# First mixer's window attention in plain fp32 on halves of TensorE's array, instead of in split fp32r pairs

## The chip, the cores and the metric

One core of one Trainium2 chip runs the whole program. The metric is the device time of one execution in microseconds (us). The kernel's engines are TensorE (PE, with its weight loads listed as PEld), VectorE (DVE), ScalarE (ACT), GpSimd (POOL) and SyncE (SP, which issues most of the DMAs).

## The reference, cut to what matters

The program is an encoder of two layers on 1024 tokens of width 1024. The first layer's token mixer is an attention in a window: 16 query heads of width 64, in four groups of four that share one key head and one value head, with a learned sink per head.

```python
def window_gqa_sink(q, k, v, sink):
    ...   # blocks of 128 tokens; each sees its own block and the one on either side (band 384)
    s = jnp.einsum('bnqhgd,bnkhd->bnhgqk', qb, kb, preferred_element_type=F32) * (d ** -0.5)
    ...
    s = jnp.where(valid[None, :, None, None], s, -jnp.inf)
    m = jnp.maximum(jnp.max(s, axis=-1, keepdims=True), sk)
    p = jnp.exp(s - m)
    p = p / (jnp.sum(p, axis=-1, keepdims=True) + jnp.exp(sk - m))
    o = jnp.einsum('bnhgqk,bnkhd->bnqhgd', p.astype(v.dtype), vb)

def mixer_window_attn(u, mem_kv, w_in, sink, w_out, pos):
    q, k, v, xq = jnp.split(u @ w_in, [...], axis=-1)
    q, k = rope(q), rope(k)
    o = window_gqa_sink(q, k, v, sink)
    return jnp.concatenate([o, memory_cross_attn(xq, mem_kv)], axis=-1) @ w_out
```

After the mixer come an output projection, a gated feed-forward part, and the second layer (a gated linear recurrence, here called `hgrn`, and another feed-forward part). All arithmetic is asked for in float32.

## The kernel before

The kernel computes float32 products on TensorE in a cheaper type, F32R, by splitting: a tile x becomes a high part h (x cast to F32R, by ACT) and a low part l = x - h (by DVE). `split` does this. `mm3` then forms h*h + h*l + l*h in three matmuls. Lines 83, 84 and 85 are these three matmuls wherever they are used, lines 88 and 89 the two halves of `split`, and lines 78 and 79 those of the weights in `wunit`. A matmul takes a stationary operand (its weight load is an instruction of its own in the trace) and streams a moving operand through it. A matmul on plain F32 tiles stands in the trace as two MATMUL records, one on F32R tiles and a transpose as one.

`window()` runs the first mixer. For each of the four groups g, `proj(g)` projects eight token tiles (`token(t)`, 24 matmuls of 384 columns each into `pj`), applies the rotation on DVE and POOL into `rq`, and turns `rq` by transposes into `ptq` (`turn`), from which the query tiles `qs` and the key tiles are made. `attend(g)` then takes eight blocks of 128 tokens. For each block and each of its four heads it forms scores in a PSUM tile `ps` (two buffers), adds the mask and takes the maximum on DVE into `sm`, takes the exponential on ACT, scales the rows by the reciprocal of the sum, transposes `sm` chunk by chunk into `pt` (two buffers), moves that to SBUF, and multiplies it with the values into `po` (one buffer). A block in the middle has 384 keys (three chunks), the first and last have 256 (two), which gives 22 chunks for a group and 88 in all. Between them run the units of the cross attention (`cross_unit`), which use the same PSUM tiles.

In the kernel before, both products of the window attention use split operands in a packed form. For the scores, a query tile holds the high part of a head on 64 rows and its low part on the other 64, the key tiles `kh` and `kl` hold the key twice, and two matmuls over all 128 rows (lines 374 and 375) give one head's scores. For the values, `v` holds the high part in 64 columns and the low part in the next 64, `ph` and `pl` are the two parts of the transposed probabilities of four heads (512 columns), and two matmuls per chunk (lines 399 and 400) give `po`, whose two halves ACT and DVE add into `o` (lines 402 and 403).

The output of groups 0 to 2 is written to DRAM (`oT`) and read back later by the output projection. That of group 3 goes by DMA into `ul` and is split from there (`split_moved`). The output projection's first part (`wo0.begin`, matmuls into `pb`) is laid beside `attend(3)`.

The order of instructions on each engine comes from a scheduler that orders the program by its own estimate of times when it is built. `tc.high_priority(n)` puts an instruction ahead of others in it, and `tc.issue_after(x)` keeps an instruction behind x. TensorE executes its matmuls in the order the scheduler gave. In `hgrn`, the lines `pe.matmul(pa[i:i + 32, c, j:j + n], ..., tile_position=(0, i))` (line 1222) already use a part of the array: 128 rows by 32 columns, in plain fp32.

Of the kernel before, what the change touches and what calls it, by code (L numbers as in the profile page):

```python
# [18 lines left out]
P = 128  # L19
# [30 lines left out]
def build(tc, A, out):  # L50
# [195 lines left out]
    def window():  # L246
# [8 lines left out]
        ap_.tile([64, 4, 256], F32, tag="o", bufs=2, name="o")  # L255
        for x, n in (("kh", 1), ("kl", 1), ("v", 1), ("qs", 8), ("ph", 2), ("pl", 2)):
            if x == "v":
                ap_.tile([P, NT, P], F32R, tag=x, bufs=n, name=x)
            else:
                ap_.tile([P, 512 if n > 1 else T], F32R, tag=x, bufs=n, name=x)  # L260
# [13 lines left out]
        def proj(g):  # L274
            us = [wunit(A["wqkv"][g, u], 768, eng=pool if u < QKV_POOL[g] else None) for u in range(4)]
            qs = [[None] * 2 for _ in range(4)]
            kvp = ap_ if g % 2 else ea
            kh = kvp.tile([P, T], F32R, tag="kh", bufs=1, name="kh")
            kl = kvp.tile([P, T], F32R, tag="kl", bufs=1, name="kl")
            v = kvp.tile([P, NT, P], F32R, tag="v", bufs=1, name="v")  # L280
            def token(t):
# [19 lines left out]
                cast = act.activation(v[:, t, :64], ps[:, 320:], AF.Copy, scale=rs0[:, t:t + 1])  # L301
                if g == 0 and t + 5 < NT:
                    tag = ("kh", "kl", "v")[t]
                    row = ap_.tile([P, NT, P] if tag == "v" else [P, T], F32R, tag=tag, bufs=1, name="row").bitcast(F32)
                    row = row.rearrange("p a b -> p (a b)") if tag == "v" else row
# [28 lines left out]
            kept = (qs, kh, kl, v)  # L334
# [12 lines left out]
        marks, moved = {}, []  # L347

        def split_moved():
            ts_ = moved.pop()  # L350
            oh, ol = uh[:, 6:8, ts_], ul[:, 6:8, ts_]
            act.copy(oh, ol.bitcast(F32))
            dve.tensor_tensor(ol, ol.bitcast(F32), oh.bitcast(F32), op=ALU.subtract)

        def attend(g, qkv, blocks=range(NT)):
            qs, kh, kl, v = qkv
            for b in range(2):
                for nn in range(4):
# [3 lines left out]
                    if nn % 2 == 0:  # L362
                        pairs[0] = ap_.tile([64, 4, 256], F32, tag="o", bufs=2, name="o")
                    o = pairs[0]
# [5 lines left out]
                    pool.tensor_copy(sm[:, :, w:w + 1], sk[:, 4 * g:4 * g + 4].unsqueeze(2))  # L370
                    for j in range(4):
                        s = psp.tile([P, 384], F32, tag="ps", bufs=2, name="ps")
                        m = slice(nn * P, (nn + 1) * P)
                        pe.matmul(s[:, :w], qs[j][b][:, m], kh[:, lo * P:hi * P], start=True, stop=False)
                        pe.matmul(s[:, :w], qs[j][b][:, m], kl[:, lo * P:hi * P], start=False, stop=True)
                        hd = 4 * g + j
                        dve.tensor_tensor_reduce(out=sm[:, j, :w], in0=s[:, :w], in1=wmask[:, mo:mo + w],
                                                 scale=-0.125, scalar=sk[:, hd:hd + 1], op0=ALU.add, op1=ALU.min,
                                                 accum_out=st["nm"][:, j:j + 1])
# [3 lines left out]
                    if moved and n % 2 == 0:  # L383
                        with tc.issue_after(marks[g, n].ins):
                            split_moved()
                    dve.reciprocal(st["rd"], st["su"])
                    for j in range(4):
                        if j < 2:
# [3 lines left out]
                    po = psp.tile([P, 4, P], F32, tag="po", bufs=1, name="po")  # L392
                    for c in range(hi - lo):
# [3 lines left out]
                        ph, pl = pair("p", c)  # L397
                        split(ph, pl, tp.rearrange("p a b -> p (a b)"))
                        pe.matmul(po, v[:, lo + c, :], ph, start=c == 0, stop=False)
                        pe.matmul(po, v[:, lo + c, :], pl, start=False, stop=c == hi - lo - 1)  # L400
                    ov = o[:, :, (nn % 2) * P:(nn % 2 + 1) * P]
                    act.copy(ov, po[64:])
                    dve.tensor_tensor(ov, po[:64], ov, op=ALU.add)
                    if nn % 2 == 1 and g == 3:
                        ts_ = slice((n - 1) * P, (n + 1) * P)
                        moved.append(ts_)
                        for hp in range(2):
                            nc.sync.dma_start(ul[hp * 64:(hp + 1) * 64, 6:8, ts_].bitcast(F32), o[:, hp::2, :])
                        if n == NT - 1:
                            split_moved()  # L410
                    elif nn % 2 == 1:
                        ts_ = slice((n - 1) * P, (n + 1) * P)
                        for hp in range(2):
                            nc.sync.dma_start(
                                oT[0][2 * g:2 * g + 2, hp * 64:(hp + 1) * 64, ts_].rearrange("a d t -> d a t"),
                                o[:, hp::2, :])
# [1166 lines left out]
```

## Time and profile before

| what | value |
|---|---|
| time, median of 3 runs | 2644.66 us (2641.44 to 2646.29) |
| the profiled execution, its span | 2644.4 us |
| PE busy over the span | 2598.7 us (98%) |
| DVE, ACT, POOL busy | 1807.8 us (68%), 1379.0 us (52%), 486.7 us (18%) |
| granted TensorE clock over 40 slices | 9 tenths or more in each |

The span of the profiled execution is 0.3 us under the median of the runs shown, so sums made against the one hold for the other. Busy time of PE is modelled from start to end of each matmul, and matmuls overlap, so the distance from one start to the next tells what a matmul costs in a stream. The window attention's own matmuls lie between 83.7 us and 493 us of the span, and the profile's views are asked for that stretch.

### The profile page before, as it was taken

Reading aid. Unit: us, or ns where it says so; the run is one execution under the profiler, and the core shown is the slowest. Engines: PE = TensorE matmul, PEld = TensorE weight load, DVE = VectorE, ACT = ScalarE, POOL = GpSimd, SP = SyncE. Lnnn points to the kernel's source line nnn. Section 1 sums busy time; section 2 is a strip of 40 time slices with the busy share of each in tenths; the row PEclk is TensorE's granted clock in tenths of the full one; section 3 lists DMA queues with packets and bytes.
Section 4 is the critical chain, followed back from the end, with each engine's and each line's share of the span. In section 5 each row is a group of like instructions: output and inputs, shape, how many; then the busy total and the mean of one; then the engine's idle time right before and its main releaser. Section 6 shows DMA issues by size and latency. Waiting matters only on the chain. (4 is left out here: it accounts for less than half of the span.)

```text
span 2644.4 us, 38978 instructions
## 1 busy us (share of the span) xinstructions
PE 2598.7 (98%) x14420; PEld 2187.7 (83%) x14420; DVE 1807.8 (68%) x2875; ACT 1379.0 (52%) x2471; POOL 486.7 (18%) x552
## 2 busy tenths in 40 slices
PE   8999999999999999999999999999999999999998
PEld 8988887887888888887888888888887788888887
DVE  6778777587656565488688686887757665656447
ACT  6667767445444444455465554555534444444443
POOL 0421120221111100032234131231311111110013
PEclk9999999999999999999999999999999999999999
DMA  9782232367877757673236351103337777785666
GB/s 354 248 191 46 74 102 69 126 190 187 210 200 197 198 158 251 201 258 127 85 112 162 85 119 47 54 32 116 121 113 191 197 196 203 202 206 166 219 193 236
DMA packets 195726, 425.92 MB, mean 161 GB/s; under 512 B 20048, under 2 KB 56272, under 8 KB 189904
## 3 DMA queue, kind: packets, MB, share of 16 engines
q1 hardware_dynamic: 161552, 324.06, 38.0%
q0 software_dynamic: 24544, 90.19, 16.5%
q10 hardware_dynamic: 9440, 9.19, 1.0%
q8 instruction: 113, 1.85, 0.3%
q14 instruction: 77, 0.63, 0.1%
HBM read 330.04 MB, written 116.39 MB: 169 GB/s over the span
## 5 line engine op out<-in xcount | busy, mean ns | idle before, releaser
L89 DVE TENSOR_TENSOR wl<-st,wh 128x1024 fp32r<-128x1024 f32 (+1 forms) x238 | 262.8, 1111 | 318.0 <-ACT wh L88 291.5
L88 ACT CAST wh<-st 128x1024 fp32r<-128x1024 f32 (+1 forms) x238 | 222.1, 935 | 286.1 <-PE X L588 186.4
L83 PE MATMUL pj<-uh,wh 128*128 128x512 f32 x512 | 202.5, 396 | 3.4 <-DVE q L1139 2.0
L588 PE MATMUL X<-wl,wh 128*128 128x512 f32 x528 | 204.7, 389 | 0.3 <-DVE wl L89 0.3
L588 PE MATMUL X<-wh,wl 128*128 128x512 f32 x528 | 204.5, 389 | 0.0
L85 PE MATMUL pj<-uh,wl 128*128 128x512 f32 x512 | 202.3, 395 | 0.0
L84 PE MATMUL pj<-ul,wh 128*128 128x512 f32 x512 | 200.9, 392 | 0.1
L588 PE MATMUL X<-wh 128*128 128x512 f32 x528 | 198.7, 390 | 0.3 <-ACT c L1002 0.3
L83 PE MATMUL pj<-wh,uh 128*128 128x384 f32 (+1 forms) x512 | 189.5, 371 | 3.7 <-DVE gs L1125 2.4
L84 PE MATMUL pj<-wl,uh 128*128 128x384 f32 (+1 forms) x512 | 187.2, 366 | 0.0
L85 PE MATMUL pj<-wh,ul 128*128 128x384 f32 (+1 forms) x512 | 187.2, 366 | 0.0
L79 DVE TENSOR_TENSOR wl<-st,wh 128x1024 fp32r<-128x1024 f32 (+1 forms) x91 | 118.3, 1305 | 33.9 <-ACT wh L78 33.3
L588 PE MATMUL V<-uh,wh 128*128 128x512 f32 x336 | 130.7, 389 | 0.0
L588 PE MATMUL V<-ul,wh 128*128 128x512 f32 x336 | 130.7, 389 | 0.0
L588 PE MATMUL V<-uh,wl 128*128 128x512 f32 x336 | 130.7, 389 | 0.0
L78 ACT CAST wh<-st 128x1024 fp32r<-128x1024 f32 (+1 forms) x97 | 97.6, 1012 | 40.9 <-PE pj L84 26.9
L588 PEld LDWEIGHTS X<-wh 128*128 128x128 f32 x528 | 99.1, 188 | 21.7 <-ACT c L1002 0.7
L588 PEld LDWEIGHTS X<-wl,wh 128*128 128x128 f32 x528 | 99.1, 188 | 20.9 <-DVE wl L89 0.8
L588 PEld LDWEIGHTS X<-wh,wl 128*128 128x128 f32 x528 | 99.1, 188 | 20.7
L83 PEld LDWEIGHTS pj<-uh,wh 128*128 128x128 f32 x512 | 96.3, 188 | 22.8 <-DVE q L1139 2.9
L971 POOL TENSOR_TENSOR c<-c,g 128x512 f32<-128x512 f32 x24 | 42.6, 1793 | 388.3 <-PE X L588 160.1
L84 PEld LDWEIGHTS pj<-ul,wh 128*128 128x128 f32 x512 | 96.2, 188 | 19.2 <-DVE ul L89 0.4
(410 smaller groups left out, 7217.6 us busy)
## 6 DMA issues: line engine op xcount, KB each, us to landing
st<-hid SPq DMA_DIRECT2D x154, 256.0 KB, 3.1
st<-in_ffw_dram SPq DMA_DIRECT2D x108, 256.0 KB, 3.2
w2s<-in_ffw_dram POOLq DMA_DIRECT2D x24, 1024.0 KB, 8.5
st<-in_ffw_dram SPq DMA_DIRECT2D x46, 512.0 KB, 4.3
hid<-tt SPq DMA_DIRECT2D x88, 256.0 KB, 4.8
st<-w2s SPq DMA_DIRECT2D x88, 256.0 KB, 3.0
sx<-in_ffw_dram SPq DMA_DIRECT2D x84, 256.0 KB, 4.0
sy<-in_ffw_dram SPq DMA_DIRECT2D x42, 512.0 KB, 6.8
```

Source lines behind the costliest of these rows:

```text
L78: act.copy(h[:, :n], raw)
L79: (eng or dve).tensor_tensor(l[:, :n], raw, h[:, :n].bitcast(F32), op=ALU.subtract)
L83: pe.matmul(o, ah, bh, start=first, stop=False)
L84: pe.matmul(o, ah, bl, start=False, stop=False)
L85: return pe.matmul(o, al, bh, start=False, stop=last)
L88: act.copy(h, src)
L89: dve.tensor_tensor(l, src, h.bitcast(F32), op=ALU.subtract)
L588: last = pe.matmul(o, x, y, start=new, stop=e, skip_group_check=not first)
L971: pool.tensor_tensor(y[q][:, t, :], y[q][:, t, :], g3[:, c], op=ALU.mult)
```

## The change

The window attention's operands are no longer split. The query tiles `qs` now hold two heads, one on rows 0 to 63 and the other on rows 64 to 127, in plain F32, and the key tile `k` holds the key on both halves. The scores of a head are one plain fp32 matmul over 64 rows (`tile_position` row 0 or 64). The scores of two heads are given the two buffers of `ps`; the head on rows 64 to 127 is written first and the other is placed behind it with high priority. The values' product takes a 64-column stationary `v` and puts two heads on columns 0 to 63 and two on columns 64 to 127, as plain fp32 matmuls of 256 columns, all chunks of a block in a row. One copy (ACT, or DVE for the middle chunk) moves a transposed chunk to SBUF as `pT`. Of the four row scalings of a block, ACT does one instead of two. `po` is copied once, or for group 3 split straight into `uh` and `ul`, without a DMA. The output of a pair of blocks goes out in one DMA instead of two.

```diff
-            qs = [[None] * 2 for _ in range(4)]
+            qs = [[None] * 2 for _ in range(2)]
...
-                cast = act.activation(v[:, t, :64], ps[:, 320:], AF.Copy, scale=rs0[:, t:t + 1])
+                cast = act.activation(v[:, t, :], ps[:, 320:], AF.Copy, scale=rs0[:, t:t + 1])
...
-                dve.scalar_tensor_tensor(v[:, t, 64:], ps[:, 320:], rs0[:, t:t + 1], v[:, t, :64].bitcast(F32),
-                                         op0=ALU.mult, op1=ALU.subtract)
...
-                        split(kh[:, hs], kl[:, hs], tp)
+                        dve.tensor_copy(kk[:, hs], tp)
                     else:
-                        lo, hi = slice(0, 64), slice(64, 128)
-                        q0, q1 = [ap_.tile([P, 512], F32R, tag="qs", bufs=8, name="qs") for _ in range(2)]
-                        qs[2 * w][b], qs[2 * w + 1][b] = q0, q1
-                        act.copy(q0[lo], tp[lo])
-                        dve.tensor_tensor(q0[hi], tp[lo], q0[lo].bitcast(F32), op=ALU.subtract)
-                        act.copy(q1[hi], tp[hi])
-                        dve.tensor_tensor(q1[lo], tp[hi], q1[hi].bitcast(F32), op=ALU.subtract)
+                        qs[w][b] = ap_.tile([P, 512], F32, tag="qs", bufs=8, name="qs")
+                        (dve.tensor_copy if w else act.copy)(qs[w][b], tp)
...
+                    scores = [None] * 4
                     for j in range(4):
-                        s = psp.tile([P, 384], F32, tag="ps", bufs=2, name="ps")
-                        m = slice(nn * P, (nn + 1) * P)
-                        pe.matmul(s[:, :w], qs[j][b][:, m], kh[:, lo * P:hi * P], start=True, stop=False)
-                        pe.matmul(s[:, :w], qs[j][b][:, m], kl[:, lo * P:hi * P], start=False, stop=True)
+                        if j % 2 == 0:
+                            scores[j:j + 2] = [psp.tile([P, 384], F32, tag="ps", bufs=2, name="ps") for _ in range(2)]
+                            mm = None
+                            for i in (1, 0):
+                                rows = slice(64 * i, 64 * i + 64)
+                                with tc.issue_after(mm.ins) if mm else nullcontext(), tc.high_priority(AHEAD if mm else 0):
+                                    mm = pe.matmul(scores[j + i][:, :w], qs[j // 2][b][rows, m], kk[rows, lo * P:hi * P],
+                                                   start=True, stop=True, tile_position=(rows.start, 0))
+                        s = scores[j]
...
-                        ph, pl = pair("p", c)
-                        split(ph, pl, tp.rearrange("p a b -> p (a b)"))
-                        pe.matmul(po, v[:, lo + c, :], ph, start=c == 0, stop=False)
-                        pe.matmul(po, v[:, lo + c, :], pl, start=False, stop=c == hi - lo - 1)
-                    ov = o[:, :, (nn % 2) * P:(nn % 2 + 1) * P]
-                    act.copy(ov, po[64:])
-                    dve.tensor_tensor(ov, po[:64], ov, op=ALU.add)
...
+                        pT = ap_.tile([P, 4, P], F32, tag="pT", bufs=3, name="pT")
+                        (dve.tensor_copy if c == 1 else act.copy)(pT, tp)
+                        pTs.append(pT)
+                    po = psp.tile([P, 2, P], F32, tag="po", bufs=1, name="po")
+                    with tc.high_priority(AHEAD):
+                        mm = None
+                        for c in reversed(range(hi - lo)):
+                            for i in range(2):
+                                with tc.issue_after(mm.ins) if mm else nullcontext():
+                                    mm = pe.matmul(po[64 * i:64 * i + 64], v[:, lo + c, :], pTs[c][:, i::2, :],
+                                                   start=c == hi - lo - 1, stop=c == 0, tile_position=(0, 64 * i))
+                    if g == 3:
+                        split(uh[:, 6:8, n * P:(n + 1) * P], ul[:, 6:8, n * P:(n + 1) * P], po)
+                        continue
...
```

The order on TensorE, in group 0 while the next group's projection (`pj`) runs beside it. First a stretch of the kernel before (L374 and L375 are the scores, L399 and L400 the values' product, L396 the transposes of probabilities, L321 those of `turn`):

```order
L374 MATMUL ps<-kh,qs 128x384
L375 MATMUL ps<-kl,qs 128x384
L399 MATMUL po<-ph,v 128x512
L374 MATMUL ps<-kh,qs 128x384
L375 MATMUL ps<-kl,qs 128x384
L400 MATMUL po<-pl,v 128x512
L396 MATMUL pt<-ident,sm 128x128 x4
L374 MATMUL ps<-kh,qs 128x384
L375 MATMUL ps<-kl,qs 128x384
```

All of these use the whole array. In the changed kernel the same place reads as follows (L363 are the scores, L393 the values' product, L383 the transposes, L316 those of `turn`):

```order
L83 MATMUL pj<-wh,uh 128x384
L363 MATMUL ps<-k,qs 128x384
L84 MATMUL pj<-wl,uh 128x384
L85 MATMUL pj<-wh,ul 128x384
L83 MATMUL pj<-wh,uh 128x384
L363 MATMUL ps<-k,qs 128x384
L84 MATMUL pj<-wl,uh 128x384
L85 MATMUL pj<-wh,ul 128x384
L393 MATMUL po<-pT,v 64x256 x6
L383 MATMUL pt<-ident,sm 128x128 x8
L363 MATMUL ps<-k,qs 128x384
L83 MATMUL pj<-wh,uh 128x384
```

The two heads of a pair, an L363 on one half of the rows and an L363 on the other, have three matmuls of the whole array between them; the six value matmuls stand together. In group 3, beside the output projection's matmuls, the pair stands together:

```order
L85 MATMUL pb<-wh,ul 128x512
L383 MATMUL pt<-ident,sm 128x128 x8
L363 MATMUL ps<-k,qs 128x384 x2
L83 MATMUL pb<-wh,uh 128x512
```

Counted over the whole order of the changed kernel, 30 of the 64 pairs stand together (20 of 384 columns and 10 of 256) and 34 are parted by 1 to 18 other matmuls (28 of 384 and 6 of 256); in group 3 it is 15 of 16 together. All 32 sets of value matmuls stand unbroken. Going along TensorE's order and leaving out those of `hgrn`, the part of the array in use changes 241 times: 97 times to a half of the rows, 32 times to a half of the columns, and 112 times to the whole array, 72 of these to an F32R matmul and 40 to a transpose. In the kernel before, these changes are none. From early in the first feed-forward part on, both orders are the same.

More of the change, by code (lines that the diff above doesn't have):

```diff
@@ L254, in window @@
         sk = ap_.tile([P, 16], F32, bufs=1, name="sk")
[L255 to L260, printed above, removed]
+        ap_.tile([P, 2, 256], F32, tag="o", bufs=2, name="o")
+        for x, n in (("k", 1), ("qs", 8), ("pT", 3)):
+            ap_.tile([P, 512 if n > 1 else T], F32, tag=x, bufs=n, name=x)
+        ap_.tile([P, NT, 64], F32, tag="v", bufs=1, name="v")
+        for x in ("ph", "pl"):
+            ap_.tile([P, 512], F32R, tag=x, bufs=2, name=x)
         ap_.tile([P, 8], F32, bufs=1, name="pad")
@@ L300, in token @@
                 sum_steps[0].send(done)
-                cast = act.activation(v[:, t, :64], ps[:, 320:], AF.Copy, scale=rs0[:, t:t + 1])
+                cast = act.activation(v[:, t, :], ps[:, 320:], AF.Copy, scale=rs0[:, t:t + 1])
                 if g == 0 and t + 5 < NT:
-                    tag = ("kh", "kl", "v")[t]
-                    row = ap_.tile([P, NT, P] if tag == "v" else [P, T], F32R, tag=tag, bufs=1, name="row").bitcast(F32)
-                    row = row.rearrange("p a b -> p (a b)") if tag == "v" else row
+                    row = ap_.tile([P, T], F32, tag="sm", bufs=3, name="row") if t else ap_.tile([P, T], F32, tag="k", bufs=1, name="row")
                     nc.sync.dma_start(row, A["x"][(t + 5) * P:(t + 6) * P, :])
@@ L345, in window @@
         pairs, roped = {}, {}
[L347 to L353, printed above, removed]
+        marks = {}
         def attend(g, qkv, blocks=range(NT)):
-            qs, kh, kl, v = qkv
+            qs, kk, v = qkv
             for b in range(2):
@@ L361, in attend @@
                         continue
-                    if nn % 2 == 0:
-                        pairs[0] = ap_.tile([64, 4, 256], F32, tag="o", bufs=2, name="o")
-                    o = pairs[0]
+                    if nn % 2 == 0 and g < 3:
+                        pairs[0] = ap_.tile([P, 2, 256], F32, tag="o", bufs=2, name="o")
                     lo, hi = max(n - 1, 0), min(n + 2, NT)
```

31 lines of the change are left out of this document (10 added, 21 removed).

## The prediction

> **What bounds the kernel now.** I read the page's busy times first, then the stretches of the mixer, then its waits.
>
> ```profile
> PE 2598.7 (98%) x14420; PEld 2187.7 (83%) x14420; DVE 1807.8 (68%) x2875; ACT 1379.0 (52%) x2471; POOL 486.7 (18%) x552
> PE 20%; DVE 1%; DMA 1%; POOL 0%; issue 0%; ACT 0%; DVEq 0%; SPq 0%; POOLq 0%; ACTq 0%
> ```
>
> TensorE is busy for 98% of the span, and what of the chain that ended last could be followed is nearly all PE. So a microsecond of PE work added or taken away counts almost in full, and one on another engine only where PE waits for it. The mixer in stretches (length, then busy time of each engine):
>
> ```profile
> core 0: us, PE busy (x) PEld busy (x) DVE busy (x) ACT busy (x) POOL busy (x), PEclk, DMA share, GB/s
> 95.00:130.00 35.00, 33.71 (x188) 29.44 (x186) 29.91 (x73) 23.80 (x57) 10.23 (x16) 1.00 0.63 209
> 130.00:200.00 70.00, 69.01 (x407) 63.10 (x405) 52.48 (x129) 49.25 (x120) 19.70 (x28) 1.00 0.84 187
> 200.00:300.00 100.00, 96.66 (x548) 85.53 (x548) 76.81 (x189) 70.53 (x169) 17.96 (x28) 0.98 0.27 65
> 300.00:400.00 100.00, 94.01 (x535) 83.12 (x534) 76.95 (x175) 68.53 (x164) 16.52 (x23) 0.98 0.28 82
> 400.00:425.00 25.00, 22.57 (x111) 17.16 (x110) 21.61 (x53) 23.58 (x55) 0.44 (x2) 1.00 0.25 75
> 425.00:495.00 70.00, 70.00 (x350) 58.76 (x349) 40.41 (x82) 36.44 (x76) 0.57 (x3) 1.00 0.20 57
> ```
>
> Here too PE leads. It lies idle for 1.3 + 1.0 + 3.3 + 6.0 + 2.4 = 14.0 us between 95 and 425 us, and not at all after that. DVE is next (52.48 + 76.81 + 76.95 + 21.61 = 228 of 295 us from 130 to 425, 77%). These 14 us are about what any relief of the other engines can return. PE's records run past the start of the next matmul, by some 0.16 us as shown below, so short waits hide in "busy", and I allow 24 us as the far end (an estimate: some 60 waits that lose 0.16 each in this way). The waits of PE and its weight loads between 80 and 460 us are short:
>
> ```profile
> PEld po L400 <- DVE pl L89: 4.5, 10, 1.3
> PEld ps L374 <- DVE nm L377: 4.5, 11, 0.7
> PEld po L399 <- ACT ph L88: 4.3, 6, 1.4
> ```
>
> They are for the split of the probabilities and for DVE to free a score buffer (us in total, times, longest).
>
> **The change on PE, scores.** Counts and what they cost in a stream:
>
> ```profile
> L374 PE MATMUL ps<-kh,qs 128*128 128x384 f32 x96 | 36.0, 377 | 1.3 <-DVE nm L377 1.0
> L375 PE MATMUL ps<-kl,qs 128*128 128x384 f32 x96 | 32.6, 341 | 0.0
> L374 PE MATMUL ps<-kh,qs 128*128 128x256 f32 x32 | 9.4, 315 | 0.3 <-DVE nm L377 0.3
> L399 PE MATMUL po<-ph,v 128*128 128x512 f32 x88 | 35.7, 406 | 3.5 <-ACT ph L88 2.8 <-ACT xo L242 0.7
> ```
>
> From the timeline (start, length in us), at 384, 256 and 512 columns:
>
> ```profile
> 194.72 0.34 PE L374 MATMUL ps<-kh,qs 128*128 128x384 f32 x1
> 194.90 0.34 PE L375 MATMUL ps<-kl,qs 128*128 128x384 f32 x1
> 195.07 0.34 PE L374 MATMUL ps<-kh,qs 128*128 128x384 f32 x1
> 195.25 0.33 PE L375 MATMUL ps<-kl,qs 128*128 128x384 f32 x1
> ```
>
> ```profile
> 271.42 0.28 PE L375 MATMUL ps<-kl,qs 128*128 128x256 f32 x1
> 271.53 0.28 PE L374 MATMUL ps<-kh,qs 128*128 128x256 f32 x1
> 271.65 0.28 PE L375 MATMUL ps<-kl,qs 128*128 128x256 f32 x1
> ```
>
> ```profile
> 267.51 0.39 PE L399 MATMUL po<-ph,v 128*128 128x512 f32 x1
> 267.74 0.40 PE L400 MATMUL po<-pl,v 128*128 128x512 f32 x1
> 267.98 0.40 PE L399 MATMUL po<-ph,v 128*128 128x512 f32 x1
> ```
>
> Starts lie 0.175 us apart at 384 columns, 0.117 at 256 and 0.233 at 512. Scores before: 192 x 0.175 + 64 x 0.117 = 41.1 us. What a plain fp32 matmul costs, and what a part of the array costs, `hgrn` shows:
>
> ```profile
> L1222 PE MATMUL pa<-E 128*32 128x32 f32 x1536 | 27.2, 199 | 0.0
> L1222 PE MATMUL pa<-E 128*32 128x64 f32 x512 | 20.5, 222 | 1.7 <-POOL E L1237 1.6
> L1297 PE MATMUL po<-S,qin 128*128 128x128 f32 x224 | 36.5, 276 | 0.0
> ```
>
> The same lines with the shortest, median and longest time of one, and the timeline around one set of L1222:
>
> ```profile
> L1222 PEld LDWEIGHTS pa<-E x2048: 106/110/113, 1245.1 to 1881.7; 128*32 128x32 f32 x187
> L1222 PE MATMUL pa<-E x2048: 192/196/243, 1245.1 to 1881.7; 128*32 128x32 f32 x140, 128*32 128x64 f32 x47
> ```
>
> ```profile
> L1273 PEld LDWEIGHTS pu<-v,kT x256: 186/192/193, 1267.0 to 1887.4; 128*128 128x128 f32 x128
> L1273 PE MATMUL pu<-v,kT x256: 270/275/377, 1267.2 to 1887.5; 128*128 128x128 f32 x128
> ```
>
> ```profile
> 1244.74 0.39 PE L83 MATMUL pj<-wh,uh 128*128 128x512 f32 x1
> 1245.06 1.17 PE L1222 MATMUL pa<-E 128*32 128x64 f32 x64
> 1246.15 0.50 PE L83 MATMUL pj<-wh,uh 128*128 128x512 f32 x1
> 1246.49 0.39 PE L84 MATMUL pj<-wl,uh 128*128 128x512 f32 x1
> ```
>
> The code issues 14 L1297 matmuls of this kind for each of 8 heads, 112, and the trace has 224: a plain fp32 matmul is two passes. From 32 to 128 columns a pass grows from 199 to 276 ns, 0.80 ns a column, against 0.45 ns for F32R (0.058 us more for 128 columns more, above); the step from 32 to 64 columns gives 0.72 and that from 64 to 128 gives 0.84. I take 0.83, so a pass of 384 columns is 0.32 us and one of 256 is 0.215, and a matmul is two of them, 0.64 and 0.43. That is nearly four times an F32R matmul. So two heads in plain fp32 cost what four split matmuls cost, if and only if they run at the same time.
>
> Do halves run at the same time? The 64 passes of a set of L1222 (16 of 64 columns, 48 of 32, on strips of 32 columns) would stream for 16 x 64 x 0.80 + 48 x 32 x 0.80 = 2.05 us one behind the other, and take 1.17. So parts of the array do overlap, when the matmuls stand together. But 34 of the 64 pairs do not: the order puts full-array matmuls between them, and PE works in order. A score alone on its half costs as much as a pair. Scores after: 20 x 0.64 + 10 x 0.43 for the pairs together, 56 x 0.64 + 12 x 0.43 for the parted, 58.1 us. That is **+17.0 us**. Ends: -3.5 if every pair overlapped (37.6 us), +34 if none did (75.2).
>
> **Values.** Before 176 x 0.233 = 41.0 us. After, 88 chunks of two halves, standing together, at 2 x 0.215: 37.8 us, **-3.2 us** (+34.6 if column halves did not overlap).
>
> **Changing the part in use.** This is what the diff does not say. Around the set of L1222, the distance into it is 0.32 us where an L83 takes 0.23; its longest pass, which I take for the first, has 243 ns where 64 columns have 222. That is 0.11 us for the entry. On the way out, the last pass starts at 1245.06 + 1.17 - 0.20 = 1246.03, and the next matmul 0.12 later where some 0.03 is due; that matmul lasts 0.50, not 0.39, and the one behind it comes after 0.34, not 0.23. So leaving costs 0.20 us. The 0.11 in it look like a weight load that is no longer hidden: the longest L1273, which can stand behind such a set, is 377 where the median is 275. Entering with 32 columns of weights (a load of 110 ns against 192 for 128 columns) shows little of it. For the row halves, with 128 columns of weights, I take 0.19 in and 0.19 out to an F32R matmul; for the column halves (64 columns) and for transposes, whose loads lie between, 0.14. Then 97 x 0.19 + 32 x 0.14 + 72 x 0.19 + 40 x 0.14 = 18.4 + 4.5 + 13.7 + 5.6 = **+42.2 us**. No row of before shows a half of the rows, so the ends are 0 and 241 x 0.20 = 48 us; I stay near the upper one because it is the nearest row, the same engine in the same precision.
>
> The Trainium skill says that changing the tiling mode, and not merely the tile within it, drains TensorE ("TensorEngine Tiling (Array Packing)", section Key Properties). The trace agrees for the one mode it has, with the 0.32 us above. By the rule all 241 changes pay, as I count them; if row halves were free of it, the sum would be that of the second rival below.
>
> **The other engines.** They give up the most instructions:
>
> ```profile
> L89 DVE TENSOR_TENSOR pl<-pt,ph 128x512 fp32r<-128x512 f32 x104 | 70.4, 682 | 18.6 <-ACT ph L88 17.2 <-PE pj L83 1.1
> L88 ACT CAST ph<-pt 128x512 fp32r<-128x512 f32 x104 | 59.7, 586 | 22.2 <-PE po L399 10.3 <-PE pt L396 6.6 <-PE po L85 4.0
> L403 DVE TENSOR_TENSOR o<-po,o 64x512 f32<-64x512 f32 x32 | 21.7, 678 | 13.6 <-ACT o L402 13.5
> ```
>
> 88 of these splits (the other 16 are the cross attention's) become one copy each, 56 on ACT and 32 on DVE, and the add into `o` one shorter copy. DVE loses 88 x 0.68 = 60 us, gains 32 copies at some 0.6 = 19, and 32 more row scalings; the query, key and `v` splits go as well. That is some tens of microseconds of 228, all beside PE's work. It is worth what PE waits for these engines: I take half of the 14 us, **-7 us** (0 to -24). The DMAs out of `o` fall from 32 to 12 on SP's queue, where the DMA share is 0.20 to 0.84; group 3's way through `ul` loses a DMA that PE, never idle after 425 us, did not wait for. Both cost and gain nothing, and are still covered if PE slows. A new wait: six value matmuls need all three `pT` of a block, so PE may stand for the last copy with full-array work queued behind it; the copies are shorter than the splits they replace, so I add nothing.
>
> **Sum.** +17.0 - 3.2 + 42.2 - 7 = +49 us on 2644.4, so 2693 us (1.9% slower; the runs' median lies 0.3 us above the span). A measurement of this kernel tells some 0.2%, 5.3 us, from no change.
>
> **Rivals.**
> 1. Relief decides, faster. If DVE and ACT set the mixer's pace through the waits that "busy" hides, and changing halves is nearly free, all 24 us return: 17.0 - 3.2 - 24 = -10 us, 2634. DVE's 77% speaks for it, PE's 94 to 99% in the same stretches against. It decides only if a change costs under 10/241 = 0.04 us, against 0.11 to 0.20 shown. Chance 0.07.
> 2. Row halves do not drain, only column halves do: 64 changes to or from these at about 0.15, 10 us: 17.0 - 3.2 + 10 - 7 = +17, 2661. For it: no row shows a row half. Chance 0.18.
> 3. The pairs that stand together do not overlap either, because the second waits for DVE to free its buffer, one maximum later. Then scores cost 75.2 us: +66, 2710. Against: counted along the order with the distances above, most of them have 2.5 us or more of PE work ahead of them since the last pair, and DVE has less to do. Chance 0.12.
> 4. Fp32 halves do not overlap at all: 34 + 34.6 + 42 - 7 = +104, 2748. The 1.17 us of L1222 speak against. Chance 0.04.
>
> The forecast has the remaining 0.59. Its own range is 2672 to 2705 (relief 0 to 24, changes 35 to 48). For 8 in 10 I go from 2655 (most of rival 2) to 2714 (rival 3), leaving out rivals 1 and 4 and the edges. Faster by over 0.2%: 0.07, all of rival 1. Within 0.2%: 0.04, the lower edge of rival 2. Slower: 0.89.
>
> **What would show it.** In the changed kernel's profile: score and value matmuls as two records each (256 and 352); passes of 384 columns about 0.5 us long (0.32 + 0.17) and 0.32 apart; both records of a pair's first passes starting together where the pair stands together; gaps of 0.1 to 0.2 us and a long first pass at each change; PE idle time falling; the mixer's values' product ending near 540 us where it ended at 493. I am wrong if the matmul behind a row half starts on time (rival 2) or if the mixer ends earlier.

## The result and the profile after

The changed kernel took 2676.05 us (median of 4 runs, 2675.52 to 2676.44), the kernel before 2645.47 us beside it (4 runs, 2641.44 to 2648.45). The ratio is 1.0118, 95% interval 1.0104 to 1.0131: slower by some 31 us. The profiled execution's span is 2674.4 us, 30.0 more than before. The forecast was 2693 us, range 2655 to 2714. The sign, the range and three of the four terms held. The fourth, the relief, was four times as large as I gave it.

The page of the changed kernel: span, busy times, and the chain that ended last.

```profile
span 2674.4 us, 38990 instructions
PE 2641.9 (99%) x14596; PEld 2162.3 (81%) x14596; DVE 1753.7 (66%) x2791; ACT 1315.7 (49%) x2347; POOL 479.9 (18%) x552
PE 22%; DVE 0%; ACT 0%; issue 0%; DVEq 0%; POOLq 0%; ACTq 0%
```

The mixer's stretches of the changed kernel, cut at the same times as before:

```profile
core 0: us, PE busy (x) PEld busy (x) DVE busy (x) ACT busy (x) POOL busy (x), PEclk, DMA share, GB/s
95.00:130.00 35.00, 34.76 (x182) 23.68 (x181) 22.40 (x56) 15.50 (x39) 8.55 (x13) 1.00 0.48 171
130.00:200.00 70.00, 70.00 (x400) 53.54 (x400) 39.34 (x98) 32.47 (x84) 22.29 (x31) 1.00 0.80 179
200.00:300.00 100.00, 100.00 (x547) 72.25 (x546) 59.90 (x154) 49.74 (x126) 17.60 (x28) 1.00 0.25 63
300.00:400.00 100.00, 99.24 (x539) 70.22 (x538) 61.81 (x158) 54.03 (x140) 8.43 (x16) 1.00 0.20 62
400.00:425.00 25.00, 25.00 (x139) 22.16 (x138) 16.29 (x27) 10.22 (x19) 6.10 (x9) 1.00 0.52 171
```

PE's idle time from 95 to 425 us is 1.0 us where it was 14.0, and the granted clock is 1.00 where two stretches had 0.98. DVE and ACT are less busy in every row shown. PE alone sets the pace now, and it has more to do.

The scores and the value product by line in the changed kernel (shortest, median and longest ns, first and last start), and scores and transposes by form:

```profile
L363 PEld LDWEIGHTS ps<-k,qs x256: 182/184/187, 85.1 to 501.6; 64*128 64x128 f32 x128
L363 PE MATMUL ps<-k,qs x256: 376/482/587, 85.1 to 501.8; 64*128 64x384 f32 x96, 64*128 64x256 f32 x32
L393 PEld LDWEIGHTS po<-pT,v x352: 132/137/137, 107.1 to 519.2; 128*64 128x64 f32 x176
L393 PE MATMUL po<-pT,v x352: 379/379/431, 107.1 to 519.4; 128*64 128x256 f32 x176
```

```profile
L363 PE MATMUL ps<-k,qs 64*128 64x384 f32 x192 | 69.7, 535 | 0.1
L383 PE MATMUL pt<-ident,sm 128*128 128x128 f32 x352 | 51.5, 277 | 0.6 <-ACT sm L376 0.6
L393 PE MATMUL po<-pT,v 128*64 128x256 f32 x352 | 45.1, 388 | 0.2 <-ACT pT L385 0.2
```

There are two records for each matmul, as forecast. A score pass lasts 0.482 us, or 0.587 where it is the first after a change of part. Its mean, 0.535, lies halfway: nearly every second pass is a first one. The last value matmul starts at 519.4 us, where L400 ended the mixer's product at 493; I had expected 540.

The timeline of the changed kernel (start, length) in group 0, where the pair is parted:

```profile
139.26 0.34 PE L83 MATMUL pj<-wh,uh 128*128 128x384 f32 x1
139.53 0.91 PE L363 MATMUL ps<-k,qs 64*128 64x384 f32 x2
140.37 0.44 PE L84 MATMUL pj<-wl,uh 128*128 128x384 f32 x1
140.65 0.34 PE L85 MATMUL pj<-wh,ul 128*128 128x384 f32 x1
140.82 0.34 PE L83 MATMUL pj<-wh,uh 128*128 128x384 f32 x1
141.09 0.91 PE L363 MATMUL ps<-k,qs 64*128 64x384 f32 x2
141.93 0.44 PE L84 MATMUL pj<-wl,uh 128*128 128x384 f32 x1
142.21 0.34 PE L85 MATMUL pj<-wh,ul 128*128 128x384 f32 x1
142.47 1.51 PE L393 MATMUL po<-pT,v 128*64 128x256 f32 x12
143.92 0.44 PE L383 MATMUL pt<-ident,sm 128*128 128x128 f32 x2
```

and in group 3, where it stands together:

```profile
447.06 0.60 PE L383 MATMUL pt<-ident,sm 128*128 128x128 f32 x4
447.59 0.92 PE L363 MATMUL ps<-k,qs 64*128 64x384 f32 x4
448.43 0.50 PE L84 MATMUL pb<-wl,uh 128*128 128x512 f32 x1
448.77 0.40 PE L85 MATMUL pb<-wh,ul 128*128 128x512 f32 x1
```

One head on its half takes 0.91 us (x2: two passes), two heads together 0.92 (x4). So halves of the rows overlap fully when they stand together, and a parted pair pays twice. The changes are to be seen as well: the score starts 0.27 us behind the L83 where the next L85 starts 0.17 behind its neighbour, and the L84 behind the score lasts 0.44 and not 0.34, with the next 0.28 behind it.

The waits view of the changed kernel, 80 to 500 us (us in total, times, longest):

```profile
PEld ps L363 <- issue: 16.2, 67, 0.4
...
PEld pj L83 <- issue: 10.0, 20, 0.5
...
PEld pj L84 <- issue: 7.8, 15, 0.5
...
PEld pt L383 <- issue: 7.4, 19, 0.5
...
PEld po L393 <- issue: 5.4, 17, 0.5
```

A change of part stands here as "issue" ahead of a weight load: it waits for no engine, 0.24 us at a time for the scores. That is how such a cost looks in a profile; PE itself reads 100% busy.

**The account.** To weigh the terms I went through PE's records from 60 us to the last value matmul. Each is taken to stream 0.417 ns a column in F32R and 0.833 ns a column for a pass of fp32, with a fixed 0.17 us behind it, which the records of before bear out (0.175 us from start to start at 384 columns). What is left between two streams I call a change where the part of the array differs, and a wait where it doesn't and the gap is over 30 ns. The clock's dips behind a wait count as waits, and a wait that falls at a change counts as part of the change. A transpose streams at the rate of an fp32 pass (0.11 us from start to start at 128 columns).

| term, us | before | after | difference | forecast |
|---|---|---|---|---|
| scores, with their share of the short gaps | 41.2 | 58.6 | +17.4 | +17.0 |
| values, the same | 40.0 | 38.1 | -1.9 | -3.2 |
| 241 changes | 0 | 45.8 | +45.8 | +42.2 |
| waits | 32.4 (85) | 1.8 (3) | -30.6 | -7 |
| sum | | | +30.7 | +49 |
| span | 2644.4 | 2674.4 | +30.0 | +49 |

### The profile page after: what moved, and what is told of

The parts are those of the page before. It is cut to its first block, busy times and chain, and to the rows that moved or that the text cites. A ratio compares the mean times of both kernels' runs of the same rounds, so it can differ in the third digit from the quotient of the medians.

```text
span 2674.4 us, 38990 instructions
## 1 busy us (share of the span) xinstructions
PE 2641.9 (99%) x14596; PEld 2162.3 (81%) x14596; DVE 1753.7 (66%) x2791; ACT 1315.7 (49%) x2347; POOL 479.9 (18%) x552
## 5 line engine op out<-in xcount | busy, mean ns | idle before, releaser
L88 ACT CAST wh<-st 128x1024 fp32r<-128x1024 f32 (+1 forms) x238 | 222.6, 937 | 291.3 <-PE X L574 193.9
L83 PE MATMUL pj<-uh,wh 128*128 128x512 f32 x512 | 203.0, 397 | 2.1 <-DVE s L1130 1.4
L85 PE MATMUL pj<-uh,wl 128*128 128x512 f32 x512 | 202.8, 396 | 0.0
L84 PE MATMUL pj<-ul,wh 128*128 128x512 f32 x512 | 201.1, 393 | 0.1
L83 PE MATMUL pj<-wh,uh 128*128 128x384 f32 (+1 forms) x512 | 191.5, 375 | 2.6 <-DVE gs L1111 2.0
L84 PE MATMUL pj<-wl,uh 128*128 128x384 f32 (+1 forms) x512 | 188.2, 368 | 0.0
L85 PE MATMUL pj<-wh,ul 128*128 128x384 f32 (+1 forms) x512 | 187.9, 367 | 0.0
L371 ACT ACTIVATE sm<-sm,nm 128x385 f32<-128x385 f32 (+1 forms) x128 | 75.2, 588 | 96.8 <-DVE nm L367 96.0
L83 PEld LDWEIGHTS pj<-uh,wh 128*128 128x128 f32 x512 | 96.3, 188 | 24.3 <-issue 3.3
L83 PEld LDWEIGHTS pj<-wh,uh 128*128 128x128 f32 x512 | 96.3, 188 | 24.0 <-issue 7.3
```

Source lines behind the costliest of these rows:

```text
L83: pe.matmul(o, ah, bh, start=first, stop=False)
L84: pe.matmul(o, ah, bl, start=False, stop=False)
L85: return pe.matmul(o, al, bh, start=False, stop=last)
L88: act.copy(h, src)
L371: marks[g, n] = act.activation(sm[:, j, :w + 1], sm[:, j, :w + 1], AF.Exp, bias=st["nm"][:, j:j + 1], scale=-1.0, accum_out=st["su"][:, j: ...
```

## The experiments

PE's costs are as forecast. Open were why nearly all waits went, and whether the changes really are paid. Two theories for the waits, called A and B where the expectations use letters: relief of the other engines (DVE above all, which no longer forms low parts) returns them; or PE itself, with 61 us more to do, comes later to each wait and finds it over. Later C and D are whether the two returns add up or fill the same waits, and D1 and D2 whether what is then left is due to the order of the values or to ACT. Each ratio is taken against runs of the kernel before beside it; the account of a run is that of its one profiled execution.

**1. Pairs together (e1_together, from after).** Both heads' scores get one PSUM tile of two banks, so no pair can be parted. The cross attention's units, which use the same buffers, get this one tile too (not shown in the cut).

```diff
-    scores[j:j + 2] = [psp.tile([P, 384], F32, tag="ps", bufs=2, name="ps") for _ in range(2)]
+    both = psp.tile([P, 2, 512], F32, tag="ps", bufs=1, name="ps")
+    scores[j:j + 2] = [both[:, 0], both[:, 1]]
```

> The changed kernel with one PSUM tile of two banks for the two heads of a pair, so that both wait for the same two maxima and all 64 pairs stand together (64 instead of 30), and the part of the array in use changes 181 times instead of 241. Theory A (the change cost PE its parted pairs and its changes of part, and the waits it took away are gone because DVE and ACT do less): scores stream 37.6 us instead of 58.6, 60 changes fewer at 0.19 us, 2676 - 21 - 11 = 2644 us, with PE's waits still a few us. Theory B (the waits are gone only because PE itself became slower): they come back in part, 10 to 20 us, 2655 to 2665.

Measured: 2664.04 us, ratio 1.0067 (1.0050 to 1.0084). By form, one place in the timeline, and two stretches of this kernel:

```profile
L365 PE MATMUL ps<-k,qs 64*128 64x384 f32 x192 | 43.9, 535 | 1.4 <-DVE nm L369 1.3
```

```profile
141.80 0.92 PE L365 MATMUL ps<-k,qs 64*128 64x384 f32 x4
```

```profile
200.00:300.00 100.00, 97.39 (x579) 74.00 (x578) 64.09 (x165) 51.71 (x134) 16.43 (x28) 1.00 0.25 66
300.00:400.00 100.00, 90.86 (x554) 71.18 (x555) 67.89 (x160) 55.95 (x139) 14.49 (x23) 1.00 0.22 68
```

The same 192 passes keep PE busy for 43.9 us and not 69.7: parting the pairs cost what was forecast. But only 12 us of the 20 came back. PE idles again: 2.6 and 9.1 us in these stretches against 0 and 0.8. Only 1.4 us of its idle time is a pair that waits for its buffers (the row above); the rest is spread over other waits for ACT and DVE. The table below counts 7 us more of waits than in after and 0.23 us for a change, where after has 0.19; so some 7 us more (181 x 0.04, an estimate) are waits that fell at a change. That makes some 15 us of waits come back, as theory B has it, and its time of 2655 to 2665 us is the one measured.

**2. and 3. One product each (e2_scores, e3_values).** Run 2 has only the scores changed, run 3 only the values' product, with its copies, scalings and output.

```diff
 # run 2: scores as after, values as before
+    pe.matmul(scores[j + i][:, :w], qs[j // 2][b][rows, m], kk[rows, lo * P:hi * P], ..., tile_position=(rows.start, 0))
 # run 3: scores as before, values as after
+    pe.matmul(po[64 * i:64 * i + 64], v[:, lo + c, :], pTs[c][:, i::2, :], ..., tile_position=(0, 64 * i))
```

> Only the scores changed, the values' product split as before; 200 changes of part (100 into row halves, 100 out), 28 pairs together. PE's own work against the kernel before: scores +19 us, changes 200 x 0.197 = +39. Theory A (waits go with DVE and ACT relief, most of which is the probabilities' split): some 10 us of the 30 return, 2645 + 58 - 10 = 2693 us. Theory B (a slower PE hides the waits by itself): nearly all 30 return, 2673 us.

> Only the values' product changed, the scores split as before; 64 changes of part (32 into column halves, 32 out). PE's own work against the kernel before: values -2 us, changes 32 x 0.145 + 32 x 0.165 = +10. Theory A: DVE and ACT lose the probabilities' split and the add, and some 25 of the 30 us of PE's waits go, 2645 + 8 - 25 = 2628 us, faster than before. Theory B: PE is hardly slower, so the waits stay, 2653 us.

Measured: scores alone 2682.09 us, 1.0139 (1.0122 to 1.0157); values alone 2634.29 us, 0.9958 (0.9943 to 0.9973). Values alone beat both kernels. Its stretches:

```profile
200.00:300.00 100.00, 99.22 (x633) 86.31 (x632) 73.67 (x191) 62.55 (x158) 17.59 (x28) 1.00 0.26 68
300.00:400.00 100.00, 94.01 (x570) 80.77 (x571) 73.41 (x167) 61.52 (x150) 14.32 (x24) 0.99 0.29 88
```

PE does some 12 us more here than before (64 changes for 13.7 us against some 2 us less of streaming), yet 20 us of waits went, while DVE and ACT are each some 3 to 8 us per 100 less busy. (Run 5 has the same 64 changes at 10.2 us, so some 3 of the 13.7 are waits, and 17 went.) That is mostly relief. In run 2, whose DVE and ACT keep the splits of the probabilities, the waits fell to 5.6 us just the same, with PE 64 us longer. That is mostly pace. Neither run is pure: run 3's PE is a little longer, and run 2 also drops the splits of the queries and keys. Runs 4 and 7 try each cause alone.

**4. Only the low part's subtraction left out (e5_relief, from before).** The low part is missing from the product, which runs twice on the high one.

```diff
-    ph, pl = pair("p", c)
-    split(ph, pl, tp.rearrange("p a b -> p (a b)"))
+    ph = pl = ap_.tile([P, 512], F32R, tag="ph", bufs=2, name="ph")
+    act.copy(ph, tp.rearrange("p a b -> p (a b)"))
```

> The kernel before with DVE's half of the probabilities' split left out (88 subtractions of 0.68 us); the second value matmul streams the high part again, so PE's matmuls are as many and as long as before, and the low part of the probabilities is missing from the result. Theory A: PE's waits shrink by 15 to 20 of some 30 us, 2627 us. Theory B: nothing but the direct wait for that subtraction (4.5 us) goes, 2641 us.

Measured: 2633.56 us, 0.9952 (0.9937 to 0.9967). DVE's 60 us of subtractions were worth some 13 us, and the waits fell by 12, from 32.4 to 20.0. That lies between the two theories: more than the direct wait, less than half of the 32 us.

**5. The whole array for the scores (e4_whole, from after).** Each head's query tile is padded with zeros to 128 rows, so scores are plain fp32 without halves: every head pays in full, but only the values change the part in use.

```diff
+    pool.memset(q[rest], 0.0)
+    (dve.tensor_copy if w else act.copy)(q[rows], tp[rows])
...
+    mm = pe.matmul(scores[j + i][:, :w], qs[j + i][b][:, m], kk[:, lo * P:hi * P], start=True, stop=True)
```

> The changed kernel with each head's query on its own half of a 128-row tile and zeros on the other half (written by POOL), so that its scores are plain fp32 over the whole array: no row halves, no pairs, and only the 64 changes of part around the values are left. If a change of part costs 0.20 us and a parted half as much as a whole: scores stream 75.6 us instead of 58.6, 194 changes at 0.198 go, 2676 + 17 - 38 = 2655 us, plus what waits come back. If the changes of part were not what is paid (the gaps at them would be waits for DVE that fall there), 2676 + 17 = 2693 us.

Measured: 2663.76 us, 1.0069 (1.0054 to 1.0084), 12 us less than after. By form in this kernel:

```profile
L365 PE MATMUL ps<-k,qs 128*128 128x384 f32 x192 | 75.3, 494 | 2.0 <-DVE nm L368 2.0
```

A pass's mean is 494 ns, near the 482 of an undisturbed one. The scores stream 16.5 us longer than in after, 177 fewer changes save 35.6, and 6 us of waits come back: -13 by the account, -12 measured. (The expectation let 194 changes go where 241 - 64 = 177 do.) So the changes are paid, row halves among them. The Trainium skill says that a change of the tiling mode drains TensorE ("TensorEngine Tiling (Array Packing)", section Key Properties). These runs agree in so far as a change costs 0.19 us; what TensorE does in that time, none of them shows.

**6. DVE's load put back (e6_load, from after).** The subtraction goes into a tile that nobody reads.

```diff
+    spare = ap_.tile([P, 4, P], F32, tag="spare", bufs=1, name="spare")
+    dve.tensor_tensor(spare, tp, pT, op=ALU.subtract)
```

> The changed kernel with DVE's subtraction put back, 88 of them at 0.68 us from the PSUM tile into a spare tile that nothing reads. Theory A (PE's waits went because DVE and ACT do less): 12 us or more of waits come back, 2688 us or more. Theory B (the slower PE gives them the time anyway): within 4 us of the changed kernel, 2676 to 2680 us.

Measured: 2686.34 us, 1.0160 (1.0143 to 1.0177). Stretches of this kernel:

```profile
200.00:300.00 100.00, 100.00 (x543) 71.68 (x543) 70.73 (x172) 49.01 (x122) 19.63 (x28) 1.00 0.26 66
300.00:400.00 100.00, 99.39 (x542) 71.71 (x541) 73.80 (x176) 52.91 (x131) 8.74 (x16) 1.00 0.17 53
```

DVE is back at 71 and 74 us per 100, and PE does not wait: 0.0 and 0.6 us idle, waits 1.9 us in all. The time still rose by 10 us in the median, and by 6.7 in the profiled execution. Some 5 of that is the order, which the added instructions altered: 260 changes and 27 pairs together, where after has 241 and 30. So the time fits neither theory and decides nothing here; the idle time does, and it is theory B's: with a longer PE and a lighter ACT, DVE's load no longer makes PE wait.

**7. and 8. A slower PE, without and with DVE's relief (e7_slowpe, e10_both, from before).** The first matmul of each score is issued three times, 41 us more for PE. Run 8 adds run 4's edit.

```diff
+    for _ in range(2):
+        pe.matmul(s[:, :w], qs[j][b][:, m], kh[:, lo * P:hi * P], start=True, stop=True)
```

> The kernel before with each head's first score matmul issued three times (the first two are overwritten by the third): PE streams 96 x 2 x 0.175 + 32 x 2 x 0.117 = 41 us more, DVE and ACT do exactly what they did. Theory A: PE's waits of some 30 us stay, 2646 + 41 = 2687 us. Theory B: most of them are filled, 20 to 28 us, 2659 to 2667 us.

> The kernel before with both: DVE's half of the probabilities' split left out (the low part of the probabilities is missing from the result), and each head's first score matmul issued three times (PE streams 41 us more). Alone, the first took some 12 us of PE's 32 us of waits and the second some 14. Theory C (each fills a part of its own, which is how the change came to lose nearly all of them): 5 us of waits left, 2646 + 41 - 27 = 2660 us. Theory D (both fill the same waits, and the rest comes from something else in the change): 2670 us or more.

Measured: 2672.06 us, 1.0105 (1.0089 to 1.0120); with relief 2674.75 us, 1.0118 (1.0103 to 1.0133). The 41 us of PE work cost 27: 14 went into waits (32.4 to 18.1), between the two theories. DVE's relief on top returns nothing, in time or in waits (19.3), as theory D has it: the two mostly fill the same waits. What is left in run 8, in its stretches and waits (us in total, times, longest):

```profile
200.00:300.00 100.00, 96.42 (x575) 90.43 (x575) 63.12 (x162) 71.41 (x172) 16.75 (x29) 0.97 0.25 61
...
400.00:425.00 25.00, 21.32 (x109) 18.55 (x108) 13.83 (x28) 11.93 (x25) 4.62 (x7) 0.86 0.31 111
```

```profile
PEld pt L398 <- ACT sm L391: 5.0, 4, 3.7
ACT kvh L196 <- DMA kvl<-kvd: 9.5, 3, 7.5
```

ACT is now the busier of the two, and the transposes wait for its row scalings. The longest of these waits, 3.7 us, has another cause behind it. ACT had stood 7.5 us, until 200.15 us of the span, for a DMA that brings the cross attention's keys and values; then it worked without a break, and this scaling came up at 202.85. PE's 3.2 us of idle time there and the clock of 0.97 in the same 100 us (3 us lost, an estimate) make some 6 of run 8's 19.3 us that go back to this DMA. In run 7 ACT waits 3.2 us for the same DMA. In the changed kernel it waits for these DMAs too, 5.9 us at the longest, and PE's idle time stays at 1.0 us.

**9. and 10. The order of the values, and ACT (e11_order, e12_act, from run 8).** Run 9 issues a block's value matmuls together behind the last chunk, as after does. Run 10 adds after's relief of ACT: one scaling of four and not two, the middle chunk's cast on DVE, and one copy out of half of `po` on DVE in place of ACT's copy and DVE's add (so half of the product is missing as well).

```diff
-    if j < 2:
+    if j < 1:
...
-    act.copy(ph, tp.rearrange("p a b -> p (a b)"))
+    (dve.tensor_copy if c == 1 else act.copy)(ph, tp.rearrange("p a b -> p (a b)"))
...
-    act.copy(ov, po[64:])
-    dve.tensor_tensor(ov, po[:64], ov, op=ALU.add)
+    dve.tensor_copy(ov, po[:64])
```

> The kernel before with less DVE and a slower PE (as in the run with both, low part of the probabilities missing), and now the values' matmuls of a block issued together behind its last chunk, last chunk first and with high priority, as the change does it (three buffers for the high part), in place of chunk by chunk. Theory D1 (the rest of PE's waits, 19 us, stood in the chain of transpose, cast and matmul chunk by chunk, which the new order breaks): waits fall under 8 us, 2663 us. Theory D2 (they are waits for ACT, whatever the order): 2672 to 2678 us.

> The run before it, with ACT's part of the change added: one row scaling of a block on ACT instead of two, the middle chunk's cast on DVE, and no ACT copy of the output (one DVE copy of one half of it, so the other half of the product is also missing from the result). Theory D1: little on top of the new order, within 4 us of it. Theory D2: waits fall from 19 us to about the 2 us of the changed kernel, 2658 us.

Measured: 2673.89 us, 1.0103 (1.0086 to 1.0120), and 2661.76 us, 1.0059 (1.0044 to 1.0074). The order alone does nothing in time or in the sum of the waits (19.8); ACT's part on top returns 12 us and brings the waits to 5.5. The stretch from 200 to 300 us and some waits, run 9 and then run 10:

```profile
200.00:300.00 100.00, 96.88 (x571) 90.80 (x570) 59.25 (x154) 65.91 (x160) 17.29 (x28) 0.97 0.25 63
PE ps L375 <- DVE nm L379: 4.6, 5, 3.1
ACT kvh L196 <- DMA kvl<-kvd: 7.7, 2, 6.2
```

```profile
200.00:300.00 100.00, 100.00 (x603) 94.03 (x602) 71.53 (x179) 58.70 (x145) 16.25 (x29) 1.00 0.26 65
ACT kvh L196 <- DMA kvl<-kvd: 0.2, 1, 0.2
```

DVE has more to do than in run 9 (71.5 against 59.3 us), ACT less, and PE's 3.1 idle us are gone. So the time is D2's, near its 2658 us. Its mechanism is shown only in part. In run 9 PE no longer waits for a row scaling: it waits for DVE's maxima, and the longest such wait, 3.1 us, stands behind the same late DMA (6.2 us of ACT, and with it of DVE). In run 10 ACT waits 0.2 us for that DMA, so some 6 of the 14 us, with the clock's dip, may be the DMA's and not ACT's. No run separates them.

**11. and 12. The best version, with work moved (e8_act2, e9_pool1, from run 3).** ACT keeps two scalings as before, or POOL takes one of DVE's three.

```diff
 # run 11
-    if j < 1:
+    if j < 2:
 # run 12
+    elif j == 3:
+        pool.tensor_scalar_mul(sm[:, j, :w], sm[:, j, :w], st["rd"][:, j:j + 1])
```

> Only the values' product changed, and ACT takes two of a block's four row scalings instead of one, as in the kernel before: DVE gives up 32 scalings of 0.43 us, ACT takes them at 0.6. Theory A (DVE is the engine that PE waits for): 3 to 5 us faster than with the values' product alone, 2630 us. Theory B (the waits for ACT's copies of the probabilities weigh as much): no change or slower, 2634 to 2640 us.

> Only the values' product changed, and POOL takes one of a block's four row scalings from DVE. Theory A: DVE gains 14 us and ACT loses nothing, 3 to 6 us faster than with the values' product alone, 2629 us. Theory B (POOL is slow at it and the transposes wait for its scaling): slower, 2640 us or more.

Measured: 2639.83 us, 0.9985 (0.9975 to 0.9995), and 2633.64 us, 0.9960 (0.9945 to 0.9974). More work for ACT costs most of run 3's gain, so in run 3, too, moving DVE's work to ACT is the wrong way, as theory B has it. POOL's help changes nothing, which neither theory forecast. Run 11 has 2 us more of waits than run 3. Its profiled execution is 2.0 us longer than that of run 3, so there the account leaves little over. That the medians lie 5.5 us apart fits with this: run 3's profiled execution, at 2638.35 us, is the slowest of its four, 4 us above their median.

**Runs 1 to 10 in the account's terms** (us, from 60 us to the last value matmul; waits and changes with their count; normal short gaps left out):

| kernel | scores stream | values stream | changes | waits | last value ends | ratio |
|---|---|---|---|---|---|---|
| before | 37.6 | 37.6 | 0 | 32.4 (85) | 493.3 | 1 |
| after | 58.6 | 38.1 | 45.8 (241) | 1.8 (3) | 519.8 | 1.0118 |
| 1 pairs together | 38.1 | 38.1 | 41.9 (181) | 9.1 (11) | 506.5 | 1.0067 |
| 2 scores only | 59.9 | 37.6 | 41.6 (200) | 5.6 (15) | 526.5 | 1.0139 |
| 3 values only | 37.6 | 38.1 | 13.7 (64) | 12.0 (24) | 476.9 | 0.9958 |
| 4 less DVE | 37.6 | 37.6 | 0 | 20.0 (49) | 475.9 | 0.9952 |
| 5 whole array | 75.1 | 38.1 | 10.2 (64) | 7.8 (13) | 503.3 | 1.0069 |
| 6 DVE loaded | 60.2 | 38.1 | 49.1 (260) | 1.9 (3) | 527.1 | 1.0160 |
| 7 slower PE | 75.1 | 37.6 | 0 | 18.1 (39) | 516.3 | 1.0105 |
| 8 both | 75.1 | 37.6 | 0 | 19.3 (50) | 517.1 | 1.0118 |
| 9 and order | 75.1 | 37.6 | 0 | 19.8 (47) | 510.2 | 1.0103 |
| 10 and ACT | 75.1 | 37.6 | 0 | 5.5 (13) | 492.9 | 1.0059 |

## Why the prediction was right, and where it was wrong

- **Scores, +17.0: right, +17.4.** Both premises hold: halves that stand together overlap (0.92 us for four passes), and parted ones pay twice. Counting 34 parted pairs in TensorE's order gave the size; run 1, without them, took it away. Rivals 3 and 4 fall with it.
- **Values, -3.2: right in sign, -1.9.** The streaming is as forecast; the rest is fewer short gaps saved.
- **Changes, +42.2: right, +45.8 for 241.** Row halves pay like the strips of `hgrn` that the price came from, and run 5 shows the price in the time. Rival 2 falls.
- **Relief, -7: wrong, -30.6. This is the mis-sized term.** It is off by 24 us, more than the whole error of 17; the other three terms came out 5 us above their forecasts and hid a part of it, which is luck. The term failed twice. The bound of 24 was too low: I counted 14 us of idle time and 60 hidden waits, where there were 85 waits and 32 us, as "busy" hides the first 0.17 us of each and the clock's dips behind the long ones. And "half" had no row behind it: I took one engine's relief as the cause, while the change brings three causes: a lighter DVE, a lighter ACT and a longer PE. DVE's relief alone takes 12 us (run 4), a slower PE alone 14 (run 7), both together leave about as much as either (run 8), and with ACT's part on top 5.5 us are left (run 10). A longer PE and a lighter ACT are enough without DVE's relief (run 6, 1.9 us left). How the 30.6 us divide between the three stays open, as some 6 us of what run 10 adds stood behind a late DMA. I had even listed L88, the cast on ACT, among the waits, and costed only DVE.
- **PE's costs count in full: right in part.** It holds for PE work put where PE doesn't wait. In the mixer a third of the new 41 us disappeared into waits (run 7).
- **DMAs and the new wait for three `pT`, nothing: not contradicted.** The changed kernel's idle time shows 0.2 us for `pT`, and run 9 shows no cost of the order. The fewer DMAs were not tried alone.
- **The range.** By its own terms (relief 24 and changes 35; relief 0 and changes 48) it is 2669 to 2706 us, not 2672 to 2705; nothing hangs on it.
- **Rival 1, faster:** its mechanism, all the hidden waits returning, came about; its condition, cheap changes, didn't. Run 3 meets the condition halfway: 64 changes in place of 241, and it is faster.

What stays open, beside the division of the 30.6 us, is small. Of the 5 us that run 1 falls short of its terms, some 4 stand behind the mixer: between 520 and 700 us its PE is busy for 175.8 us where after has 178.2, and the clock there is 0.94 and 0.98 in two stretches of 20 us where after has 1.00. Run 6 is busy for the same 175.8 us, with 0.91 in one such stretch. Why, no run shows.

## What to carry to other kernels

Before a matmul goes onto a part of the array, count in the engine's order how often the part in use changes and which partners stand together: each change cost 0.19 us here and a parted partner its full time, together more than all the waits that went. A term for waits needs a bound from the gaps between streams, not from idle time. Ask for it which engines are relieved, whether the longer PE work fills the same waits anyway, and what the engine named in a wait was itself waiting for: in run 8 it was a DMA. Where a change has two halves, try each: the values' half alone was 0.4% faster, the scores' half alone 1.4% slower.

## What the runs showed of the hardware

The price of a change differs little between the parts. In the changed kernel it is some 0.20 us into row halves (0.27 for 0.17 and 0.587 for 0.482 in the rows above), 0.15 into column halves (0.26 for 0.17 and 0.431 for 0.379), 0.20 out to an F32R matmul (0.09 between the streams, and 0.44 for 0.34) and 0.15 out to a transpose (0.09, and 0.44 for two where 0.27 + 0.11 is due). That column halves are cheaper goes with their shorter weight loads (137 against 184 ns), which no run separates.

A wait of PE can cost more than itself, because behind some waits the clock drops. In the kernel before:

```profile
386.98 0.41 PE L321 MATMUL ptq<-ident,rq 128*128 128x128 f32 x2 [1.94 <-DVE kl L89]
...
388.55 0.43 PE L321 MATMUL ptq<-ident,rq 128*128 128x128 f32 x1 [0.93 <-POOL rq L299]
...
390.06 0.63 PE L83 MATMUL pb<-wh,uh 128*128 128x512 f32 x1
390.49 0.63 PE L84 MATMUL pb<-wl,uh 128*128 128x512 f32 x1
...
393.28 0.39 PE L84 MATMUL pb<-wl,uh 128*128 128x512 f32 x1
393.51 0.39 PE L85 MATMUL pb<-wh,ul 128*128 128x512 f32 x1
```

After idle times of 1.94 and 0.93 us, matmuls of 512 columns stand 0.43 us apart and not 0.23, for about 3 us. In run 8 the stretch with 3.7 idle us has a granted clock of 0.86; in after, which hardly waits, the clock is 1.00 in every stretch shown. Not every wait does it: run 1 idles 9.1 us between 300 and 400 us, in waits of 1.9 us at most, at a clock of 1.00. What decides, no run here separates.
